# A decoder step on one core: layer 0's second token half by seven block products in 19 of its 22 FFN slices, their operand sums in tiles that attention outputs held, those outputs through DRAM, and the memory tokens loaded one stage earlier

## The chip, the core and the metric

The kernel runs on one NeuronCore of a Trainium2 chip. The metric is the device time of one execution in microseconds (us); lower is better. Five engines run their own instruction lists in order and wait for each other by semaphores: PE (TensorE, matmuls and transposes; "PEld" in the profile is its weight loading), DVE (VectorE), ACT (ScalarE), POOL (GpSimd, which here issues copies from DRAM to DRAM) and SP (SyncE, which issues nearly all other DMAs).

## What is computed

One inference step of a two-layer decoder over two groups of tokens with the same weights: a prompt of 1024 tokens and 8 sample tokens. The width is 1024, everything is float32.

```python
for l in (0, 1):
    hn = rmsnorm(h, g[0])
    # layer 0: gated linear recurrence; layer 1: stick-breaking attention over a shared K/V
    # both: in parallel with cross-attention into 256 memory tokens
    mix = concat(mixer(hn), mem_attend(q_m, mem_k[l], mem_v[l])) @ w_o[l]
    h = h + rmsnorm(mix, g[1])
    h = h + rmsnorm(swiglu(rmsnorm(h, g[2]), w_gu[l], w_down[l]), g[3])
    if l == 0:                                  # shared K/V, used by layer 1
        sb_k, sb_v = split(rmsnorm(h, g_kv) @ w_kv)
# swiglu(x) = (silu(x @ w_gate) * (x @ w_up)) @ w_down, hidden width 22 * 128 = 2816
```

The memory keys and values are projected from `mem_prompt` for both layers. Outputs are the hidden states of both groups, the recurrent states, the shared K/V and the memory K/V.

## The kernel before

**Tiles.** Activations lie transposed, channels on the 128 partitions and tokens along the free dimension. The prompt is cut in two halves: group 0 has 512 tokens, group 1 has 512 plus the 8 sample tokens, 520 columns taken as two pieces of 260. A float32 product is made of three matmuls in a reduced format (fp32r): each operand is split into a high part, rounded by ACT, and a low part, the remainder from DVE (`split_w`, lines 206 and 207, for weights; `split_to` for activations), and high*high, high*low and low*high are summed in PSUM.

**Two ways to make an FFN slice.** The hidden width is worked in 22 slices of 128, numbered 0 to 21 and grouped into five parts of 5, 5, 4, 4 and 4 (`PARTS`). A slice needs a gate and an up projection over 1024 channels, then SiLU and a product; at the end of a part the down projection adds its share to `R`.

- Plain (class `ffn`, through `proj`, line 220; or `gate_up_q`, line 464, inside `ffn_w`): for each of gate and up, 8 channel blocks by 3 terms by 2 pieces, 96 matmuls a slice.
- Seven block products (`gate_up_w`, line 511): the 2 x 2 block form by Strassen's scheme in Winograd's variant. The channels are halved, the tokens are halved, gate and up are the two output blocks. Seven products of 4 channel blocks by 3 terms, 84 matmuls a slice, on sums of weights and sums of activations. Four PSUM banks `pa`, `pb`, `pc`, `pd` (one buffer each) hold the partial sums, and ACT copies a partial sum with its sign turned from `pa` to `pb` after the first product and from `pb` to `pc` after the third. The weight sums of a part are made ahead in DRAM by POOL's accumulating DMAs (`weight_sums`, lines 549 to 569): 16 for a part, in two runs of eight of which most must wait for an earlier one to land. Each is preceded by a tiny POOL copy (`mk`) that reads the tile in `now[0]`; it paces the DMAs by the work. The activation sums are made by `sums_w` in 16 steps during the first slices of the class, which are plain (the `steps` argument); a slice by products needs 7 weight tiles split, a plain one 4.

SiLU is done either by ACT's `Silu` (in `gate_up_q` and `gate_up_w`) or as Exp, Ln, Exp and a DVE product (`silu`, lines 237 to 241). The second form needs no other function table than the softmax and the stick-breaking attention do.

**Order.** The program is one sequence of Python generators. `weave` advances several of them in turn, each in proportion to the number given with it; a scheduler then orders each engine's list, and tiles come from pools with a fixed number of buffers, so that a new tile waits until the last reader of an old one is through. The stages that matter here, in the main part at the end of `tile_decoder`:

1. `a0.v()` and `a0.fq()` project for group 0; then `a0.core()`, the recurrence, is woven with `mem_load()` (memory tokens transposed and split, lines 796 to 814), the memory keys and values of both layers, and `a0.qm`.
2. Later, `f0.finish`, `kv_proj(0)`, `b0.heads()` and `o1.finish()`: end of layer 0 for group 0, shared K/V, layer 1's queries for group 0, and the residual and norm that give group 1 its FFN input `o1.x` (while `o1.R` keeps the same values unsplit).
3. `b0.sb()` and `b0.mem()`, layer 1's two attentions of group 0, woven with parts 0 and 1 of group 1's layer 0 FFN by class `ffn`, plain. The attention outputs go to the eight `xo` tiles taken by `b0.open()` from pool `xpool` (tag `x0`, 8 buffers) and are split there (lines 911, 912, 1404, 1405).
4. `set_banks(True)` changes PSUM from two double banks to four single ones, and `ffn_w(1, 0, ...)` makes parts 2 to 4: slices 10 to 12 plain, slices 13 to 21 by products. Its operand sums lie in pool `apool`.
5. `o0.mm(b0.xo, ...)`: the output projection of layer 1 for group 0.

Layer 1's own weight sums (`ws`) are spread over many of these stages.

Of the kernel before, what the change touches and what calls it, by code (L numbers as in the profile page):

```python
# [9 lines left out]
F32 = mybir.dt.float32  # L10
# [8 lines left out]
P = 128  # L19
# [4 lines left out]
def tile_decoder(  # L24
# [11 lines left out]
    H = 4  # L36
# [189 lines left out]
    def split_to(dst, src):  # L226
        nc.scalar.copy(dst[0], src)  # L227
        nc.vector.tensor_sub(dst[1], src, dst[0].bitcast(F32))  # L228

    def silu(dst, ps, g):  # L230


        n = NG[g]
        x = T()
        dst = T() if dst is None else dst
        d = dst[:, :n]
        nc.vector.tensor_scalar(sv(x, g), pv(ps, g), -44.0, None, op0=ALU.max)  # L237
        nc.scalar.activation(d, x[:, :n], AF.Exp, scale=-1.0)
        nc.scalar.activation(d, d, AF.Ln, bias=1.0)
        nc.scalar.activation(d, d, AF.Exp, scale=-1.0)  # L240
        nc.vector.tensor_mul(d, d, x[:, :n])
        return dst
# [35 lines left out]

    def sums_w(g, xs, ops, YT, ZT):

# [4 lines left out]
        for k in range(4):  # L285
# [14 lines left out]

            b11, b12, b21, b22 = full(x0, 0), full(x0, h), full(x1, 0), full(x1, h)
            for d, p, a, b in (
# [148 lines left out]

    def gate_up_q(g, l, f, xt, side, n_side, first):

# [3 lines left out]
        for j in range(2):  # L457
# [14 lines left out]
            for a in range(2):  # L472
                d = sg[:, a * h : (a + 1) * h]
                if j == 0:
# [6 lines left out]

    def gate_up_w(g, l, f, ops, spl, raws):

# [39 lines left out]
        sg = T()  # L523
        nc.scalar.activation(sg[:, :h], pa[:, :h], AF.Silu)
        product(pb, 4)
        dt = T()
        nc.scalar.copy(dt[:, h:n], pd[:, :h])
        gt = T()
        nc.vector.tensor_add(gt[:, h:n], dt[:, h:n], pb[:, :h])
        product(pc, 5)  # L530
        nc.vector.tensor_sub(gt[:, :h], pc[:, :h], dt[:, h:n])
        product(pb, 6)
        act[0] = nc.scalar.activation(sg[:, h:n], gt[:, :h], AF.Silu)
        nc.vector.tensor_mul(sg[:, :h], sg[:, :h], pb[:, :h])  # L534
# [40 lines left out]
    class ffn_w:  # L575


        def __init__(self, g, l, x, steps, first, rows, R=None, own=False):
# [3 lines left out]
            self.half = []  # L582

            def YT():
# [6 lines left out]
            self.sums = sums_w(g, x, self.ops, YT, YT if rows else lambda: A(F32R))  # L591

        def spl(self):
            self.n += 1
            if (self.pi or not self.rows) and not self.own and self.n % 8 in (1, 4, 6):
                return cpool.tile([P, 2, 512], F32R, tag="c", name=nm("ws"))
# [8 lines left out]
        def raws(self):  # L605
            self.r += 1
            if not self.rows and self.r % 2:
                return B().rearrange("p (k m) -> p k m", k=4)
# [7 lines left out]
        def part(self, pi):  # L616
# [5 lines left out]
            for j in range(nf):  # L622
                self.pi = pi
                if f0 + j < self.plain:
                    mids.append(
                        gate_up_q(g, l, f0 + j, self.x, self.sums, self.steps[j], PARTS[self.first][0])
                    )
                    now[0] = mids[-1][:, 0, 0:1].bitcast(F32)
                else:
                    mids.append(gate_up_w(g, l, f0 + j, self.ops, self.spl, self.raws))  # L630
                yield
# [232 lines left out]
    def mem_attn(g, l, qm, xo):  # L864
# [4 lines left out]
        for h in range(H):  # L869
            po = S()  # L870
            for pr in range(2):
# [38 lines left out]
                yield  # L910
            d = xo[H + h]
            split_to((d[:, 0, :G], d[:, 1, :G]), po)

# [426 lines left out]
    def sb_prompt(g, Qs, xo):  # L1340
# [49 lines left out]
        for h in range(H):  # L1390
# [12 lines left out]
            values(vh, po, *late)  # L1403
            d = xo[h]
            split_to((d[:, 0, :G], d[:, 1, :G]), po)

# [17 lines left out]
    class mixer_b:  # L1424
# [6 lines left out]

        def open(self):
            self.xo = wo_tiles(self.g)

# [40 lines left out]
    with tc.issue_after(made[0].ins):  # L1475
# [160 lines left out]
```

## Time and profile before

| | |
|---|---|
| time, median of 3 runs | 2454.28 us (2452.27 to 2455.25) |
| the profiled execution | 2454.5 us, its span 2452.8 us |
| PE busy | 2413.3 us, 98% of the span, 15839 matmuls recorded |
| DVE, ACT, POOL busy | 1639.9, 1252.4 and 187.0 us |
| DMA | 397.40 MB, mean 162 GB/s; SP's queue 43.2%, POOL's 14.2% of the span of 16 DMA engines |
| granted TensorE clock | 0.998 |

The 1.7 us between the profiled execution's time and its span lie around the program. In a row of a timeline the first number is the start from the span's start, the second the length of a merged group, the number after "x" the count; text in square brackets tells how long the engine was idle before and what released it. A group can be drawn longer than the distance to the next one, since matmuls overlap: times between starts are the ones to use. In a row of groups stand busy time, mean ns of one instruction, and idle time before it. In a row of windows stand, for each engine, busy time and number of instructions, then the granted clock, the DMA share and GB/s. An engine with a "q" (SPq) is that engine's queue of issuing instructions.

### The profile page before, as it was taken

The numbers are of one execution on the slowest core, as the hardware profiler recorded it, in microseconds if no ns is written. First come the engines' busy times: TensorE is split into PE (matmuls) and PEld (weight loads), VectorE is DVE, ScalarE is ACT, GpSimd is POOL, SyncE is SP. The second block draws the span as 40 slices with busy tenths as digits, with TensorE's granted clock in tenths as the row PEclk, the third lists the DMA queues.
The fourth block names the chain that finished last, engine by engine and source line by source line (L and its number), as shares of the span: only waits on it lengthen the run. The fifth ranks groups of instructions, "written<-read, shape, count | busy, mean of one in ns | idle before, by whom it ended". The sixth has DMA issues, their size and how long they took to land.

```text
span 2452.8 us, 42098 instructions
## 1 busy us (share of the span) xinstructions
PE 2413.3 (98%) x15839; PEld 2161.2 (88%) x15839; DVE 1639.9 (67%) x2987; ACT 1252.4 (51%) x2441; POOL 187.0 (8%) x315
## 2 busy tenths in 40 slices
PE   8999999999999999999999999999999999999998
PEld 6888889888879988999999989877777888999998
DVE  5766557665797686664756685788688467755565
ACT  5547644354445554555434554555554445654445
POOL 1000101111000000111200102121000100000000
PEclk9999999999999999999999999999999999999999
DMA  6354676567645447676766649745354563464542
GB/s 190 100 174 110 157 197 161 135 171 204 204 137 166 132 147 235 176 188 161 190 172 168 199 132 291 206 146 154 95 164 120 145 191 116 144 194 141 151 143 74
DMA packets 534733, 397.40 MB, mean 162 GB/s; under 512 B 21325, under 2 KB 473018, under 8 KB 534530
## 3 DMA queue, kind: packets, MB, share of 16 engines
q1 hardware_dynamic: 505346, 315.02, 43.2%
q0 software_dynamic: 29184, 79.70, 14.2%
q8 instruction: 124, 2.03, 0.3%
q14 instruction: 79, 0.65, 0.1%
HBM read 364.81 MB, written 101.14 MB: 190 GB/s over the span
## 4 chain that ended last, share of the span: by engine, by line
PE 84%; DVE 6%; DMA 5%; issue 2%; ACT 2%; POOL 0%; SPq 0%; DVEq 0%; ACTq 0%; POOLq 0%
PE mm L220 44%; PE q L511 13%; PE q L648 9%; PE q L464 3%; PE mm L1042 2%; PE s L1188 1%; DMA c<-in_cache_mem_v 1%; PE s L1385 1%; PE s L906 1%; PE mm L824 1%; PE mm L851 1%; PE q L680 1%; PE s L1351 1%; PE s L875 1%; DVE ws L207 1%
## 5 line engine op out<-in xcount | busy, mean ns | idle before, releaser
L220 PE MATMUL mm<-x,ws 128*128 128x260 f32 (+1 forms) x6240 | 1113.6, 335 | 4.9 <-DVE t L237 1.7
L220 PEld LDWEIGHTS mm<-x,ws 128*128 128x128 f32 x6240 | 941.8, 188 | 125.8 <-issue 2.4
L206 ACT CAST ws<-w 128x512 fp32r<-128x512 f32 (+1 forms) x652 | 382.3, 588 | 489.5 <-PE mm L220 337.0
L207 DVE TENSOR_TENSOR ws<-w,ws 128x512 fp32r<-128x512 f32 (+1 forms) x652 | 418.9, 648 | 246.8 <-ACT ws L206 241.7
L220 PE MATMUL mm<-m,ws 128*128 128x512 f32 (+1 forms) x1344 | 281.8, 361 | 0.1
L220 PEld LDWEIGHTS mm<-m,ws 128*128 128x128 f32 x1344 | 217.9, 189 | 36.8 <-issue 1.0
L648 PE MATMUL q<-m,ws 128*128 128x260 f32 (+1 forms) x1824 | 221.8, 283 | 0.0
L648 PEld LDWEIGHTS q<-m,ws 128*128 128x128 f32 x1824 | 218.9, 188 | 1.2 <-DVE t L534 0.4
L502 DVE TENSOR_TENSOR ws<-w,ws 128x512 fp32r<-128x512 f32 x181 | 124.0, 690 | 86.6 <-ACT ws L501 83.6
L501 ACT CAST ws<-w 128x512 fp32r<-128x512 f32 x181 | 111.8, 621 | 110.2 <-PE q L648 35.6
L511 PE MATMUL q<-x,ws 128*128 128x260 f32 (+1 forms) x1188 | 158.1, 282 | 0.0
L511 PEld LDWEIGHTS q<-x,ws 128*128 128x128 f32 x1188 | 148.7, 188 | 0.0
L511 PE MATMUL q<-y,ws 128*128 128x260 f32 x912 | 119.7, 284 | 0.4 <-ACT q L521 0.3
L511 PEld LDWEIGHTS q<-y,ws 128*128 128x128 f32 x912 | 113.7, 189 | 0.8 <-ACT q L521 0.5
L464 PE MATMUL q<-x,ws 128*128 128x260 f32 (+1 forms) x720 | 91.3, 284 | 0.2 <-DVE r L400 0.2
L464 PEld LDWEIGHTS q<-x,ws 128*128 128x128 f32 x720 | 88.4, 189 | 1.8 <-DVE r L400 0.5
L511 PE MATMUL q<-a,ws 128*128 128x260 f32 (+1 forms) x672 | 87.0, 282 | 0.0
L511 PEld LDWEIGHTS q<-a,ws 128*128 128x128 f32 x672 | 83.2, 188 | 0.0
L657 DVE TENSOR_TENSOR r<-r,q 128x260 f32<-128x260 f32 (+1 forms) x128 | 48.5, 420 | 50.5 <-PE q L648 50.5
L237 DVE TENSOR_SCALAR t<-mm 128x512 f32<-128x512 f32 (+1 forms) x58 | 40.1, 691 | 48.0 <-PE mm L220 47.8
L563 POOL COPY mk<-a 128x1 f32<-128x1 f32 x36 | 21.3, 592 | 645.5 <-ACT a L1241 392.9
L228 DVE TENSOR_TENSOR m<-t,m 128x512 fp32r<-128x512 f32 (+1 forms) x88 | 60.8, 691 | 9.4 <-ACT m L227 8.7
(355 smaller groups left out, 3029.5 us busy)
## 6 DMA issues: line engine op xcount, KB each, us to landing
w<-in_w_gu SPq DMA_DIRECT2D x297, 256.0 KB
w<-in_w_down SPq DMA_DIRECT2D x160, 256.0 KB
wsum<-in_w_gu POOLq DMA_DIRECT2D x72, 512.0 KB, 6.6
w<-wsum SPq DMA_DIRECT2D x104, 256.0 KB
w<-in_w_in_a SPq DMA_DIRECT2D x80, 256.0 KB
w<-in_w_o SPq DMA_DIRECT2D x64, 256.0 KB
wsum<-in_w_gu POOLq DMA_DIRECT2D x24, 640.0 KB, 7.3
wsum<-wsum POOLq DMA_DIRECT2D x24, 512.0 KB, 5.7
```

The costliest lines, as they stand in the source:

```text
L206: nc.scalar.copy(ws[:, 0, :n, :], raw[:, :n, :])
L207: nc.vector.tensor_sub(ws[:, 1, :n, :], raw[:, :n, :], ws[:, 0, :n, :].bitcast(F32))
L220: nc.tensor.matmul(ps[:, a, : PW[g]], wt, xt[k][:, xi, o : o + PW[g]], start=(k == 0 and wi == 0), stop=(k == nk - 1 and wi == 2),)
L228: nc.vector.tensor_sub(dst[1], src, dst[0].bitcast(F32))
L237: nc.vector.tensor_scalar(sv(x, g), pv(ps, g), -44.0, None, op0=ALU.max)
L464: ins = nc.tensor.matmul(pp[a][:, :h], wt, xt[k][:, xi, a * h : (a + 1) * h], start=(k == 0 and wi == 0), stop=(k == ND - 1 and wi == 2),)
L501: nc.scalar.copy(w[:, 0, :], src)
L502: nc.vector.tensor_sub(w[:, 1, :], src, w[:, 0, :].bitcast(F32))
L511: nc.tensor.matmul(ps[:, :h], w[:, wj, k * P : (k + 1) * P], x[:, xi, :], start=(first and k == 0 and wi == 0), stop=(k == 3 and wi == 2), ...
L648: nc.tensor.matmul(pp[a][:, :h], wt, mids[k][:, xi, a * h : (a + 1) * h], start=(k == 0 and wi == 0), stop=(k == nf - 1 and wi == 2),)
L657: nc.vector.tensor_add(d, d, pp[a][:, :h])
L1042: nc.tensor.matmul(pb[i][:, a, :], xt[k][:, xi, c * P : (c + 1) * P], ws[:, s, :], start=(k == 0 and wi == 0), stop=(k == ND - 1 and wi == 2),
```

## The change

Group 1's layer 0 FFN is now made by `ffn_w` throughout: slices 0 to 2 plain by `gate_up_q`, slices 3 to 21 by seven products, so that ten slices (3 to 12) change from 96 to 84 matmuls and need 7 instead of 4 weight splits. What that takes:

- Weight sums of layer 0's parts 0 and 1 (`w1`): 32 more DMAs by POOL of 640 KB each, issued while `f0.finish`, `kv_proj(0)` and `b0.heads()` run.
- The single PSUM banks hold from the start of stage 3 on. The first two parts run beside the attentions (`beside=(0, 1)`). There the SiLU takes the form with Exp and Ln (`lean`), where it works on both token halves at once after the sixth product, and weight tiles come from `wraw` and `wspl` alone (5 buffers each).
- The activation sums are made in place from `o1.R` (`src`), without the 16 additions of `full`, and lie in the eight `x0` tiles.
- Group 0's attention outputs therefore go unsplit to DRAM (`put`: an ACT copy, a store by SP), and `mixer_b.load` brings them back and splits them during the last down projection.
- `mem_load()` is woven with `a0.fq()`, one stage earlier.

```diff
+    def put(xo, i, cols, src):
+        if isinstance(xo, list):
+            split_to((xo[i][:, 0, cols], xo[i][:, 1, cols]), src)
+            return
+        t = B()[:, : cols.stop - cols.start]
+        nc.scalar.copy(t, src)
+        nc.sync.dma_start(xo[:, i, cols], t)
...
     # sums_w(..., src=None)
+            if src:
+                b11, b12, b21, b22 = (src[i][:, c : c + h] for i in (k, k + 4) for c in (0, h))
+            else:
+                b11, b12, b21, b22 = full(x0, 0), full(x0, h), full(x1, 0), full(x1, h)
...
+    def gated(d, x):
+        nc.scalar.activation(d, x, AF.Exp, scale=-1.0)
+        nc.scalar.activation(d, d, AF.Ln, bias=1.0)
+        nc.scalar.activation(d, d, AF.Exp, scale=-1.0)
+        nc.vector.tensor_mul(d, d, x)
...
     # gate_up_q(..., lean=False)
+                if j == 0 and lean:
+                    if a == 0:
+                        x = T()
+                    nc.vector.tensor_scalar(x[:, a * h : (a + 1) * h], pp[a][:, :h], -44.0, None, op0=ALU.max)
+                    if a:
+                        gated(sg[:, :n], x[:, :n])
+                elif j == 0:
...
     # gate_up_w(..., lean=False)
         product(pa, 3)
         sg = T()
+        if lean:
+            nc.vector.tensor_scalar(sg[:, :h], pa[:, :h], -44.0, None, op0=ALU.max)
+        else:
+            nc.scalar.activation(sg[:, :h], pa[:, :h], AF.Silu)
         product(pb, 4)
         dt = T()
+        if lean:
+            gt = dt
+            nc.scalar.copy(dt[:, :h], pd[:, :h])
+            nc.vector.tensor_add(gt[:, h:n], dt[:, :h], pb[:, :h])
+            product(pc, 5)
+            nc.vector.tensor_sub(sg[:, h:n], pc[:, :h], dt[:, :h])
+            nc.vector.tensor_scalar(sg[:, h:n], sg[:, h:n], -44.0, None, op0=ALU.max)
+            x, sg = sg, T()
+            product(pb, 6)
+            gated(sg[:, :n], x[:, :n])
...
         nc.vector.tensor_mul(sg[:, :h], sg[:, :h], pb[:, :h])
         nc.vector.tensor_mul(sg[:, h:n], sg[:, h:n], gt[:, h:n])
...
     # ffn_w(..., beside=(), src=None)
-                if rows:
+                if rows or beside:
                     return xpool.tile([P, 2, NG[1]], F32R, tag="x0", name=nm("y"))
...
     # mem_attn
-            d = xo[H + h]
-            split_to((d[:, 0, :G], d[:, 1, :G]), po)
+            put(xo, H + h, slice(0, G), po)
     # sb_prompt
-            d = xo[h]
-            split_to((d[:, 0, :G], d[:, 1, :G]), po)
+            put(xo, h, slice(0, G), po)
...
+        def load(self):
+            d, n, self.xo = self.xo, NG[self.g], []
+            for k in range(ND):
+                t = T()
+                nc.sync.dma_start(t[:, :n], d[:, k, :n])
+                x = X(self.g)
+                split_to((x[:, 0, :n], x[:, 1, :n]), t[:, :n])
+                self.xo.append(x)
+                yield
...
-    drain(a0.v(), a0.fq())
+    drain(a0.v())
+    weave((a0.fq(), 8), (mem_load(), 2))
     weave(
         (a0.core(), 22),
-        (chain(mem_load(), mem_keys(0), mem_values(0), mem_keys(1), mem_values(1), a0.qm(M)), 22),
+        (chain(mem_keys(0), mem_values(0), mem_keys(1), mem_values(1), a0.qm(M)), 20),
     )
...
+    w1 = weight_sums(0, (0, 1))
     drain(o1.mm(a1.xo, 0, 1))
-    weave((f0.finish(True), 9), (o1.mm(a1.xo, 1, 5), 4))
-    weave((normed(0, f0.R, f0.r, gkvcol, xk0, True), 8), (o1.mm(a1.xo, 5, 7), 2))
-    drain(kv_proj(0, xk0))
-    weave((normed(0, f0.R, f0.r, lambda k: gcol(1, 0, k), xb0), 8), (o1.mm(a1.xo, 7, ND), 1))
+    weave((f0.finish(True), 9), (o1.mm(a1.xo, 1, 5), 4), (islice(w1, 8), 9))
+    weave((normed(0, f0.R, f0.r, gkvcol, xk0, True), 8), (o1.mm(a1.xo, 5, 7), 2), (islice(w1, 4), 5))
+    weave((kv_proj(0, xk0), 8), (islice(w1, 10), 11))
+    weave((normed(0, f0.R, f0.r, lambda k: gcol(1, 0, k), xb0), 8), (o1.mm(a1.xo, 7, ND), 1), (islice(w1, 4), 5))
     b0 = mixer_b(0, xb0)
-    weave((b0.heads(), 8), (o1.finish(), 17), (islice(ws, 4), 4))
-    b0.open()
+    weave((b0.heads(), 8), (o1.finish(), 17), (w1, 6))
+    b0.open(True)
+    set_banks(True)
+    fw = ffn_w(1, 0, o1.x, (5, 6, 5), 0, False, beside=(0, 1), src=o1.R)
+    weave((chain(b0.sb(), b0.mem()), 25), (chain(fw.part(0), fw.part(1)), 18), (islice(ws, 34), 35))
+    p4 = fw.part(4)
+    weave((chain(fw.part(2), fw.part(3), islice(p4, 4)), 20), (islice(ws, 12), 12))
+    weave((p4, 4), (b0.load(), 8))
     f1 = ffn(1, 0, o1.x)
-    weave((chain(b0.sb(), b0.mem()), 25), (chain(f1.part(0), f1.part(1)), 18), (islice(ws, 34), 35))
-    set_banks(True)
-    fw = ffn_w(1, 0, o1.x, (5, 6, 5), 2, False, f1.R)
-    weave((chain(fw.part(2), fw.part(3), fw.part(4)), 24), (islice(ws, 8), 8))
-    f1.acc = fw.acc
+    f1.R, f1.acc = fw.R, fw.acc
     set_banks(False)
```

More of the change, by code (lines that the diff above doesn't have):

```diff
@@ L575, in tile_decoder, with __init__ @@
     class ffn_w:
-        def __init__(self, g, l, x, steps, first, rows, R=None, own=False):
+        def __init__(self, g, l, x, steps, first, rows, R=None, own=False, beside=(), src=None):
             self.g, self.l, self.x, self.ops, self.steps, self.rows, self.own = g, l, x, [], steps, rows, own
@@ L582, in __init__ @@
             self.half = []
+            self.beside = beside
             def YT():
-                if rows:
+                if rows or beside:
                     return xpool.tile([P, 2, NG[1]], F32R, tag="x0", name=nm("y"))
@@ L589, in YT @@
                 return A(F32R)
-            self.sums = sums_w(g, x, self.ops, YT, YT if rows else lambda: A(F32R))
+            self.sums = sums_w(g, x, self.ops, YT, YT if rows or beside else lambda: A(F32R), src)
         def spl(self):
             self.n += 1
-            if (self.pi or not self.rows) and not self.own and self.n % 8 in (1, 4, 6):
+            if (self.pi or not self.rows) and not self.own and self.pi not in self.beside and self.n % 8 in (1, 4, 6):
                 return cpool.tile([P, 2, 512], F32R, tag="c", name=nm("ws"))
@@ L606, in raws @@
             self.r += 1
-            if not self.rows and self.r % 2:
+            if not self.rows and self.pi not in self.beside and self.r % 2:
                 return B().rearrange("p (k m) -> p k m", k=4)
@@ L625, in part @@
                     mids.append(
-                        gate_up_q(g, l, f0 + j, self.x, self.sums, self.steps[j], PARTS[self.first][0])
+                        gate_up_q(
+                            g, l, f0 + j, self.x, self.sums, self.steps[j], PARTS[self.first][0], pi in self.beside
+                        )
                     )
```

30 lines of the change are left out of this document (14 added, 16 removed).

## The prediction

> **What bounds the kernel now.** I read the page first: the span, the busy shares, and the chain of work that ended last.
>
> ```profile
> span 2452.8 us, 42098 instructions
> ...
> PE 2413.3 (98%) x15839; PEld 2161.2 (88%) x15839; DVE 1639.9 (67%) x2987; ACT 1252.4 (51%) x2441; POOL 187.0 (8%) x315
> ...
> PE 84%; DVE 6%; DMA 5%; issue 2%; ACT 2%; POOL 0%; SPq 0%; DVEq 0%; ACTq 0%; POOLq 0%
> ```
>
> PE is busy 98% of the span, and 84% of the last chain is PE. Whoever takes matmuls away shortens the kernel, as long as the other engines still deliver. The second view is the table of windows over the stretches that the change touches: the start with the memory tokens, the stretch that gets the new weight sums, stage 3 (attentions beside parts 0 and 1), parts 2 to 4, and a later stretch; the last row is a stretch of it that is full of POOL's sums.
>
> ```profile
> 0.00:300.00 300.00, 284.82 (x1723) 247.97 (x1724) 198.52 (x423) 171.38 (x353) 19.85 (x56) 0.99 0.50 143
> ...
> 852.00:998.00 146.00, 144.73 (x831) 124.39 (x832) 103.87 (x170) 74.97 (x132) 5.32 (x8) 1.00 0.61 182
> 998.00:1216.00 218.00, 217.34 (x1686) 207.11 (x1686) 133.31 (x262) 113.33 (x230) 35.00 (x65) 1.00 0.71 174
> 1216.00:1411.00 195.00, 194.72 (x1622) 194.08 (x1620) 114.16 (x211) 91.06 (x175) 18.71 (x27) 1.00 0.67 187
> 1411.00:1560.00 149.00, 145.69 (x1011) 133.96 (x1012) 106.41 (x177) 75.86 (x134) 24.05 (x36) 1.00 0.77 217
> ...
> 1005.00:1105.00 100.00, 99.51 (x780) 93.98 (x779) 60.11 (x108) 54.79 (x106) 16.08 (x32) 1.00 0.71 179
> ...
> 1471.00:1533.00 62.00, 60.81 (x480) 58.46 (x480) 34.81 (x61) 27.06 (x47) 13.09 (x22) 1.00 1.05 292
> ```
>
> In stage 3 PE idles 0.66 us of 218, in parts 2 to 4 0.28 of 195: there is nothing to win there but matmuls, and any new wait is paid in full. At the start PE idles 15.2 us of 300.
>
> **Matmuls.** The third view is PE's timeline: a piece of a plain slice woven with attention, then a plain slice and a slice by seven products in parts 2 to 4.
>
> ```profile
> 1129.31 8.14 PE L220 MATMUL mm<-x,ws 128*128 128x260 f32 x65
> 1137.29 1.03 PE L875 MATMUL s<-c,a 128*128 128x256 f32 x4
> ...
> 1221.75 28.86 PE L464 MATMUL q<-x,ws 128*128 128x260 f32 x240
> 1250.44 1.60 PE L511 MATMUL q<-x,ws 128*128 128x260 f32 x12
> ...
> 1283.72 1.61 PE L511 MATMUL q<-x,ws 128*128 128x260 f32 x12
> 1285.16 3.04 PE L511 MATMUL q<-a,ws 128*128 128x260 f32 x24
> ...
> 1293.79 1.59 PE L511 MATMUL q<-x,ws 128*128 128x260 f32 x12
> ```
>
> Start to start, a woven matmul takes (1137.29 - 1129.31) / 65 = 0.1228 us, an unwoven plain one (1250.44 - 1221.75) / 240 = 0.1195. One product, 12 matmuls, takes 1285.16 - 1283.72 = 1.44 us, and a slice by products (1293.79 - 1283.72) = 10.07 us for 84. Slices 3 to 12 lose 12 matmuls each, 120 in all, and the order of the two kernels' instructions on PE shows exactly 120 fewer. That is -14.4 us at 0.12; if the woven matmuls (some 590 in seven slices) also came down from 0.1228 to 0.1195, -2 more. I take **-15** (-14.4 to -17).
>
> **Memory tokens.** The waits of PE at `mem_load` and just behind it:
>
> ```profile
> 87.77 0.63 PE L807 MATMUL ns<-ident,c 128*128 128x128 f32 x4 [2.60 <-DVE memt L228]
> ...
> 89.06 2.93 PE L1168 MATMUL s<-b,a 128*128 128x192 f32 x8 [0.66 <-ACT b L1164]
> ...
> 93.02 0.51 PE L824 MATMUL mm<-memt,ws 128*128 128x256 f32 x2 [0.46 <-ACT memt L227]
> 93.72 1.22 PE L824 MATMUL mm<-memt,ws 128*128 128x256 f32 x8 [0.19 <-DVE memt L228]
> ```
>
> The transposes wait for the splits of the ones before. Woven with `a0.fq()` they have projection matmuls ahead of them in PE's list. The four waits add to 3.9 us; the 16 transposes only move, and the splits lie beside matmuls. What could be late next is the 0.66 that has an ACT instruction of the recurrence behind it, so I take **-3** (0 to -3.9).
>
> **The new form of SiLU.** This is where the change can lose. In a slice by products in parts 2 to 4 the sixth partial sum leads to one DVE subtraction and one ACT `Silu`, then two DVE products free the banks:
>
> ```profile
> 1292.55 0.43 DVE L531 TENSOR_TENSOR t<-q,t 128x260 f32<-128x260 f32 x1
> ...
> 1293.13 0.42 ACT L533 ACTIVATE t<-t 128x260 f32<-128x260 f32 x1
> ...
> 1294.20 0.42 DVE L534 TENSOR_TENSOR t<-t,q 128x260 f32<-128x260 f32 x1
> ...
> 1295.42 0.37 ACT L518 ACTIVATE q<-q 128x260 f32<-128x260 f32 x1
> ```
>
> Bank `pb` is read last by the first product (L534 before, 571 after), and the next slice's sign copy (L518 before, 541 after) must write `pb`, which the next slice's third product needs. Before, the reader starts 1.65 us after the subtraction and no wait of PE follows. In the seven slices of parts 0 and 1 (3 to 9) that reader is instead behind a longer chain. The durations, from the groups by form:
>
> ```profile
> L531 DVE TENSOR_TENSOR t<-q,t 128x260 f32<-128x260 f32 x28 | 12.0, 428 | 2.6 <-PE q L511 1.9
> ...
> L524 ACT ACTIVATE t<-q 128x260 f32<-128x260 f32 x28 | 10.8, 387 | 16.2 <-PE q L511 16.2
> ...
> L239 ACT ACTIVATE t<-t 128x512 f32<-128x512 f32 x32 | 20.2, 632 | 1.0
> ...
> L241 DVE TENSOR_TENSOR t<-t,t 128x512 f32<-128x512 f32 x32 | 22.1, 689 | 24.4 <-ACT t L240 24.4
> ...
> L501 ACT CAST ws<-w 128x512 fp32r<-128x512 f32 x181 | 111.8, 621 | 110.2 <-PE q L648 35.6 <-PE q L511 25.8 <-DMA w<-wsum 18.7
> L502 DVE TENSOR_TENSOR ws<-w,ws 128x512 fp32r<-128x512 f32 x181 | 124.0, 690 | 86.6 <-ACT ws L501 83.6 <-DMA w<-wsum 1.1 <-DMA w<-in_w_down 0.4
> ```
>
> After the sixth product (`pc`): subtraction 0.43, clamp (an SBUF operation, between 0.35 and 0.43; 0.35), Exp, Ln, Exp at 0.63 each on all 520 columns, the product of sigmoid and gate 0.69, the product with `pb` 0.43, the sign copy 0.37: 4.16. One weight cast of ACT (0.62) will stand between two of them, since casts keep coming: 4.78; nine hand-overs between engines at about 0.1 (1293.13 less the 1292.98 at which L531 ends is 0.15) make 5.7. What PE has meanwhile is the seventh product and the next slice's first two, 3 x 1.44, and, woven in, part of an attention unit, about 0.4: 4.7. So PE waits about **1.0** at each hand-over, and there are seven: slice 3 to 4, 4 to the down projection, 5 to 6, 6 to 7, 7 to 8, 8 to 9, 9 to the down projection. That is **+7**. The low end is 0: the weave can put a score product of 1.03 us there. The high end is a queue on ACT and DVE: the softmax's exponentials stand in the same ACT list, and so does their accumulator reading.
>
> ```profile
> L886 ACT ACTIVATE b<-s,nmx 128x256 f32<-128x256 f32 x64 | 29.9, 471 | 18.0 <-DVE nmx L880 17.8
> ...
> L886 ACT ACTIVATION_READ_ACCUMULATOR b<-s,nmx 128x1 f32 x64 | 12.6, 197 | 0.0
> ...
> L892 DVE TENSOR_SCALAR b<-b,sme 128x256 f32<-128x256 f32 x64 | 19.9, 352 | 0.7
> ```
>
> Two of these with their readings, 1.34, and a further cast, 0.62, add 1.9 to the 1.0: 2.9 at each, +20. I keep 0 to 20.
>
> **The plain slices 0 to 2.** The sums are made here: 16 steps of a subtraction (0.43) and a split (its DVE half as long) are 13.7 us of DVE in three slices of 96 x 0.1228 = 11.8 plus 1.7 of attention, 40.5 us. DVE is busy 0.60 of the row 1005 to 1105, 24.3 of 40.5; with the sums 38.0, 94%. It fits, barely. And there are fewer PSUM buffers for scores now, since the first gate pieces take two of the tag `S`. I take **+2** (0 to 5, the high end being three waits for a softmax round of 0.47 + 0.20 + 0.35 with its scores' hand-overs, about 1.6 each).
>
> **The weight sums `w1`.** 32 DMAs of 640 KB enter 852 to 998, where 4 sum DMAs of `ws` go out. A run of eight by POOL, with the queue's totals:
>
> ```profile
> q0 software_dynamic: 29184, 79.70, 14.2%
> ...
> 1466.68 0.60 POOL L568 DMA_DIRECT2D wsum<-in_w_gu  x1 [0.27 <-issue]
> ...
> 1498.59 0.87 POOL L566 DMA_DIRECT2D wsum<-in_w_gu  x1 [3.31 <-DMA wsum<-wsum]
> ```
>
> Eight take 32 us, four runs 128: from 852 they end at about 980. Slice 3 needs the first two runs at 998 + 40 = 1038, slice 5 the other two at about 1100. Late sums are thus unlikely. But the stretch fills: its 0.61 of 146 us is 89 us of DMA, and 28 more DMAs at 14.2% of 2452.8 us over 120 sum DMAs (2.9 us each) add 81, 170 of 146. The row 1471 to 1533 shows such a stretch, share 1.05 and 292 GB/s, and there PE idles 1.19 of 62 us, 1.9%; over 146 us that is 2.8, against 1.27 there now. So **+2** (0 to 6; the overflow mostly drags the sums, which have time).
>
> Parts 0 and 1 also ask SP for 21 more weight tiles of 256 KB, 5.5 MB, in the stage at 174 GB/s: some 38 more, 212, no more than 1411 to 1560 carries (217).
>
> **Outputs through DRAM.** `put` is an ACT copy and a store in place of an ACT copy and a DVE remainder of 0.69: DVE gains 8 x 0.69. `load` makes eight casts and eight remainders, 8 x (0.62 + 0.69) = 10.5 us on two engines, beside a last down projection of 192 x 0.12 = 23 us: 0 (0 to 2, the last tile's landing and split if it trails).
>
> **Slices 10 to 12 by products** behave like slices 13 to 21 now, which have no PE wait to speak of (0.28 us of 195): nothing beside their 36 matmuls. Their sums are in place before.
>
> **Sum,** against the profiled execution's own 2454.5 us (span 2452.8 and 1.7 around it; the median of the runs is 2454.28, 0.2 less): -15 - 3 + 7 + 2 + 2 = -7, 2447.5; on the median's scale **2447**.
>
> **Rivals.**
> 1. *Nothing is lost.* Hand-overs, sums and DMA stay hidden: 2454.5 - 18 = 2436.5. For it: PE's 0.4 of attention at each hand-over is an estimate and may be a whole unit. Against it: the chain of 5.7 us is longer than the three products in any case.
> 2. *All is eaten.* 1.7 at each hand-over (one more cast and some queueing), 3 in the plain slices, 3 from DMA: 12 + 6 = 18, so 2454.5. For it: DVE at 94% there.
> 3. *Slower.* At each of the seven hand-overs the sign copy on ACT or the product on DVE stands behind a whole softmax or stick-breaking round. Even with gain 18 and 4 elsewhere, it turns at (18 - 4) / 7 = 2.0 us each; with 3.3 (the 2.9 above and DVE's 0.35 of L892) it is 7 x 3.3 + 4 = 27, +9, 2463.5. For it: ACT and DVE run in list order, so one early attention instruction that waits for PE holds the chain, and PE waits for the chain. Against it: ACT is busy only 0.55 of 1005 to 1105.
> 4. *The clock falls.* If short waits between groups made the granted clock 0.75 through seven slices of 10.07: 7 x 10.07 x (1 / 0.75 - 1) = +23.5, about 2470. The windows speak against it: 0.99 in 0 to 300 with 15.2 us of idle PE, 1.00 in 1411 to 1560 with 3.3. The Trainium skill, "TensorE: Matmul & The Clock Gate", section "A second HAM failure mode: psum-queue depth-cycling", tells of a kernel whose PE idled briefly between groups while it cycled through PSUM banks, and whose clock swung between half and full rate; by that rule this form, which cycles four banks, would be such a case. The parts 2 to 4 cycle the same four banks at 1.00, so the trace bears it out only for a PE that doesn't wait.
>
> That the change doesn't do what it says is excluded for the matmuls by the count of 120.
>
> **How the numbers follow.** Forecast 0.54 (hand-overs at 0 to 1.6 each, 2439 to 2451); nothing lost 0.10; all eaten 0.18; slower 0.15; clock 0.02; late sums or something else 0.01. The range 2437 to 2461 takes the forecast, the eaten case, nearly all of the first and a part of the third. About 0.2%, 4.9 us, is what a measurement of this kernel can tell from no change: faster is below 2449.4, slower above 2459.2. The forecast gives 0.49 to faster and 0.05 to the middle, rival 1 all to faster, rival 2 most to the middle (0.01 to slower): faster 0.59, same 0.22, slower 0.19.
>
> **What would show it.** In the profile after: 120 fewer matmuls; no wait on `memt`; slices 3 to 9 at 10.1 us plus attention, with PE's waits on the sign copy (ACT, line 541) about 1 us at each hand-over, and those of the plain slices 2 us together; POOL's last `w1` sum before 1038; PE's idle time in 852 to 998 below 4 us; eight `load` splits before the output projection's first matmul; the granted clock at 1.00. Waits of 2 us and more at line 541 would make it wrong upwards, none would make it wrong downwards.

## The result

The changed kernel takes 2481.65 us (median of 6 runs, 2477.54 to 2487.32) where the kernel before takes 2455.08 in the same comparison: a ratio of 1.0109 (95% interval 1.0094 to 1.0124), 26.6 us slower. The forecast was 2447, with a range up to 2461. The profiled execution, 2487.3 us with a span of 2485.5, was the slowest of the six, so distances within its trace are a few microseconds larger than those between medians.

The page of the changed kernel, the lines that answer to those shown of before:

```profile
span 2485.5 us, 42261 instructions
...
PE 2414.0 (97%) x15719; PEld 2156.4 (87%) x15719; DVE 1658.7 (67%) x3049; ACT 1278.4 (51%) x2517; POOL 228.2 (9%) x379
...
q0 software_dynamic: 35840, 100.68, 17.5%
...
PE 79%; DMA 8%; DVE 7%; ACT 3%; issue 3%; SPq 1%; POOL 0%; DVEq 0%; ACTq 0%; POOLq 0%
```

The 120 matmuls are gone (15839 to 15719), yet PE's busy time is the same, 2414.0 us after 2413.3; and the idle time has grown from 39.5 to 71.5 us. So the remaining matmuls have become slower, by 0.7 + 14.4 = 15 us in all (120 matmuls at 0.12 us are the 14.4). The mean granted clock agrees, 0.991 after 0.998. DMA's share of the last chain has gone from 5% to 8%.

Where it went is read by four landmarks on PE's timeline, which both kernels have: the group of 227 matmuls after group 0's first FFN, the first score matmuls of the attentions, the first matmul of slice 10, and the output projection of layer 1. Of the kernel before:

```profile
858.87 27.31 PE L220 MATMUL mm<-x,ws 128*128 128x260 f32 x227
...
997.60 1.03 PE L1351 MATMUL s<-a,a 128*128 128x128 f32 x4
...
1216.02 5.89 PE L464 MATMUL s<-x,ws 128*128 128x260 f32 x48
...
1411.61 5.80 PE L220 MATMUL mm<-x,ws 128*128 128x512 f32 x24 [0.90 <-DVE r L657]
```

and of the changed kernel:

```profile
851.80 27.31 PE L220 MATMUL mm<-x,ws 128*128 128x260 f32 x227
...
1012.09 1.03 PE L1390 MATMUL s<-a,a 128*128 128x128 f32 x4
...
1236.54 2.66 PE L534 MATMUL q<-x,ws 128*128 128x260 f32 x12 [2.56 <-DVE r L697]
...
1440.52 5.77 PE L220 MATMUL mm<-x,ws 128*128 128x512 f32 x24 [0.90 <-DVE r L697]
```

| stretch, us | before | changed | difference | forecast |
|---|---|---|---|---|
| start to the 227 matmuls | 858.9 | 851.8 | -7.1 | -3 |
| 227 matmuls to the attentions (where `w1` is made) | 138.7 | 160.3 | +21.6 | +2 |
| attentions to slice 10 (parts 0 and 1) | 218.4 | 224.5 | +6.0 | -10.3 matmuls, +7, +2 |
| slice 10 to the output projection (parts 2 to 4) | 195.6 | 204.0 | +8.4 | -4.3 |
| the rest | 1041.2 | 1045.0 | +3.8 | 0 |

The windows of the changed kernel over the second, third and fourth stretch, and over 13 us of the second:

```profile
852.00:1012.00 160.00, 142.22 (x778) 119.55 (x777) 103.10 (x172) 73.64 (x131) 31.03 (x54) 0.96 0.98 268
1012.00:1236.00 224.00, 213.78 (x1606) 202.43 (x1604) 140.53 (x297) 129.11 (x283) 36.20 (x68) 0.98 0.85 219
1236.00:1440.00 204.00, 196.11 (x1584) 194.27 (x1584) 124.46 (x234) 100.76 (x196) 22.60 (x32) 0.97 0.72 198
...
955.00:968.00 13.00, 4.69 (x14) 3.22 (x15) 1.35 (x4) 0.62 (x1) 2.51 (x4) 0.61 1.07 341
```

The DMA share of the second stretch is 0.98 (0.61 before). In 955 to 968 all 16 DMA engines are busy, PE works 4.69 of 13 us, and the granted clock there is 0.61. PE's waits in this stretch, from the view of waits:

```profile
PE ns L391 <- DMA ht<-in_x_prompt: 9.5, 2, 6.8
PE ns L264 <- ACT n L227: 6.7, 3, 3.3
```

The first is the prompt's rows arriving late from DRAM (issued at 955.4 to 957.7, 7.9 us to land). The second names ACT; but ACT's own list shows what held it ahead of PE's waits at 950 and 990, casts of weight tiles that had not landed:

```profile
946.69 0.62 ACT L206 CAST ws<-w 128x512 fp32r<-128x512 f32 x1 [6.15 <-DMA w<-in_w_in_b]
...
987.85 0.62 ACT L206 CAST ws<-w 128x512 fp32r<-128x512 f32 x1 [3.46 <-DMA w<-in_w_in_b]
```

The issues by line of that stretch give these weights a median of 13.4 us from issue to landing:

```profile
w<-in_w_in_b SPq DMA_DIRECT2D x16, 256.0 KB, 13.4
```

**So the first theory (A)** was: the weight-sum DMAs fill the DMA engines, what SP loads comes late, engines that work their lists in order pass the delay on, and PE pays twice, by the wait and by a slower clock behind it. **The rival (B)**, the forecast's own fear, was the chain of the new SiLU at the hand-overs between slices and the fuller lists of DVE and ACT.

### The profile page after: what moved, and what is told of

It is laid out like the page before. It is cut to its first block, busy times and chain, and to the rows that moved or that the text cites. A ratio compares the mean times of both kernels' runs of the same rounds, so it can differ in the third digit from the quotient of the medians.

```text
span 2485.5 us, 42261 instructions
## 1 busy us (share of the span) xinstructions
PE 2414.0 (97%) x15719; PEld 2156.4 (87%) x15719; DVE 1658.7 (67%) x3049; ACT 1278.4 (51%) x2517; POOL 228.2 (9%) x379
## 4 chain that ended last, share of the span: by engine, by line
PE 79%; DMA 8%; DVE 7%; ACT 3%; issue 3%; SPq 1%; POOL 0%; DVEq 0%; ACTq 0%; POOLq 0%
PE mm L220 36%; PE q L534 16%; PE q L688 10%; PE q L481 3%; DMA w<-in_w_in_b 2%; PE s L1227 1%; PE mm L1081 1%; DVE ws L207 1%; PE s L946 1%; PE s L1424 1%; DMA w<-in_w_gu 1%; PE mm L891 1%; PE mm L864 1%; PE q L720 1%; PE s L1390 1%
## 5 line engine op out<-in xcount | busy, mean ns | idle before, releaser
L220 PE MATMUL mm<-x,ws 128*128 128x512 f32 (+1 forms) x5280 | 993.5, 344 | 4.1 <-DVE r L697 1.7
L220 PEld LDWEIGHTS mm<-x,ws 128*128 128x128 f32 x5280 | 825.1, 189 | 123.7 <-DVE x L228 2.1
L206 ACT CAST ws<-w 128x512 fp32r<-128x512 f32 x612 | 357.5, 586 | 469.5 <-PE mm L220 279.2
L207 DVE TENSOR_TENSOR ws<-w,ws 128x512 fp32r<-128x512 f32 x612 | 391.5, 645 | 253.2 <-ACT ws L206 246.6
L688 PE MATMUL q<-m,ws 128*128 128x260 f32 (+1 forms) x2304 | 290.2, 286 | 9.1 <-DVE r L697 9.1
L688 PEld LDWEIGHTS q<-m,ws 128*128 128x128 f32 x2304 | 282.4, 191 | 12.9 <-DVE r L697 7.2
L534 PE MATMUL q<-y,ws 128*128 128x260 f32 x1824 | 246.1, 286 | 3.3 <-ACT q L541 3.1
L525 DVE TENSOR_TENSOR ws<-w,ws 128x512 fp32r<-128x512 f32 x241 | 165.5, 690 | 117.8 <-ACT ws L524 115.1
L534 PEld LDWEIGHTS q<-y,ws 128*128 128x128 f32 x1824 | 230.5, 190 | 5.1 <-ACT q L541 4.4
L220 PE MATMUL mm<-m,ws 128*128 128x512 f32 x864 | 219.8, 402 | 0.7 <-DVE r L411 0.7
L524 ACT CAST ws<-w 128x512 fp32r<-128x512 f32 x241 | 148.8, 619 | 135.1 <-PE q L688 40.1
L603 POOL DMA_DIRECT2D wsum<-in_w_gu x80 | 73.0, 924 | 163.1 <-DMA wsum<-wsum 124.6
L228 DVE TENSOR_TENSOR m<-t,m 128x512 fp32r<-128x512 f32 (+1 forms) x88 | 60.8, 690 | 10.1 <-ACT m L227 8.5
```

Source lines behind the costliest of these rows:

```text
L206: nc.scalar.copy(ws[:, 0, :n, :], raw[:, :n, :])
L207: nc.vector.tensor_sub(ws[:, 1, :n, :], raw[:, :n, :], ws[:, 0, :n, :].bitcast(F32))
L220: nc.tensor.matmul(ps[:, a, : PW[g]], wt, xt[k][:, xi, o : o + PW[g]], start=(k == 0 and wi == 0), stop=(k == nk - 1 and wi == 2),)
L524: nc.scalar.copy(w[:, 0, :], src)
L525: nc.vector.tensor_sub(w[:, 1, :], src, w[:, 0, :].bitcast(F32))
L534: nc.tensor.matmul(ps[:, :h], w[:, wj, k * P : (k + 1) * P], x[:, xi, :], start=(first and k == 0 and wi == 0), stop=(k == 3 and wi == 2), ...
```

## The experiments

**One part alone, on the kernel before.**

Memory tokens, with `weave((a0.fq(), 8), (mem_load(), 2))` and nothing else:

> The kernel before with one edit: the memory tokens woven with a0.fq(). All theories: the four PE waits of 3.9 us at the memory tokens go, and the clock that the profile shows at 0.99 in the first 300 us goes back to 1.00, so 4 to 7 us faster than before, some 2448 us. If the 7.1 us that the changed kernel is ahead at the end of group 0's first FFN came from elsewhere, it would be faster by less than 3.

Measured: 2448.53 us, ratio 0.9973 (0.9960 to 0.9985). So the 7 us are this move. Its window of the first 300 us:

```profile
0.00:300.00 300.00, 289.00 (x1748) 251.31 (x1749) 198.97 (x425) 172.90 (x357) 23.17 (x62) 1.00 0.52 149
```

PE is idle 11.0 us there after 15.2, so 4.2 of the 7 are the waits. The clock reads 1.00 after 0.99: before, it was 0.84 in 86 to 90 us and 0.73 in 90 to 94, and 1.00 in both with the move. PE was busy 1.57 and 3.35 us of these, so an estimated 0.16 x 1.57 + 0.27 x 3.35 = 1.2 us more. In the traces the 227 matmuls start 5.7 us earlier.

Weight sums, issued as in the changed kernel and read by nobody:

```diff
+    w1 = weight_sums(0, (0, 1))
...
-    weave((f0.finish(True), 9), (o1.mm(a1.xo, 1, 5), 4))
+    weave((f0.finish(True), 9), (o1.mm(a1.xo, 1, 5), 4), (islice(w1, 8), 9))
...
```

> The kernel before with one edit: the 32 weight-sum DMAs of parts 0 and 1 are issued where the changed kernel issues them (and ws is spread as there), though nothing reads them. Theory A (the DMA engines are full in that stretch; weights and prompt rows come late, PE waits, and the granted clock falls after each wait): 16 to 24 us slower than before, about 2475, with the loss between the end of group 0's FFN and the start of the attentions. Rival B (the hand-overs between slices and the fuller DVE and ACT lists cost the time): within 3 us of before.

Measured: 2477.78 us, ratio 1.0090 (1.0072 to 1.0108), 22 us slower. The trace is of the fastest of the four runs, 17 us longer than that of before:

```profile
859.11 27.31 PE L220 MATMUL mm<-x,ws 128*128 128x260 f32 x227
...
1014.12 1.14 PE L1351 MATMUL s<-a,a 128*128 128x128 f32 x4 [0.17 <-DMA a<-ksc]
```

The stretch before the attentions takes 155.0 us, 16.3 more than before, and the next stretch 218.5, as before: the loss is where theory A put it. B is out for this part, since no slice has changed.

Half of these sums, 16 at half the pace:

> The kernel before with the weight-sum DMAs of part 0 alone, 16 in place of 32, at half the pace over the same stages; nothing reads them. Theory A in its form with a threshold (PE waits only where the DMA engines are full, and 0.61 of 146 us and 12 more DMAs of 2.9 us stay at 0.85): 0 to 5 us slower than before, 2455 to 2460. In its form without one (each sum DMA costs its share, 22 us for 32): 11 us slower, about 2466.

Measured: 2460.02 us, ratio 1.0015 (1.0004 to 1.0026), some 4 us (1 to 6 by the interval). Sixteen cost some 4 and thirty-two 22, so the price isn't proportional to the count. Whether there is a threshold, two counts can't tell. The same window as in the forecast, in the traces of the half and of the whole change:

```profile
852.00:998.00 146.00, 144.23 (x827) 123.28 (x825) 102.76 (x168) 74.89 (x132) 21.14 (x31) 1.00 0.84 236
```
```profile
852.00:998.00 146.00, 128.22 (x718) 108.15 (x717) 89.30 (x147) 64.82 (x115) 27.45 (x50) 0.95 1.00 275
```

At a share of 0.84 PE works 144.23 of 146 us, at 1.00 it works 128.22. The half does lose something just behind this window: PE's first score matmuls wait 2.88 us at 999.8 for keys from DRAM (`a<-ksc`).

Attention outputs through DRAM (`put` and `load`, with the weave of the last part):

> The kernel before with one edit: the attention outputs go through DRAM and are loaded back and split during the last down projection. Theory A, whose second part is that a split waits on ACT for its load and holds the next weight splits and the additions to R behind it: 5 to 10 us slower than before, with one PE wait of 4 us or more at the last down projection. Rival B: within 2 us of before.

Measured: 2461.04 us, ratio 1.0022 (1.0010 to 1.0034), 5.6 us slower by the medians; slice 10 to the output projection takes 201.2 us after 195.6. The wait at the last projection is 2.63, smaller than expected, and 144 matmuls behind it take 20.30 us, where 144 x 0.12 is 17.3.

**The changed kernel with fewer or other sums.**

18 of the 32 sums one stage earlier, woven with `rest()`:

> The changed kernel with 18 of the 32 weight-sum DMAs moved one stage earlier, beside layer 0's group 0 FFN, and 14 left where they were. Theory A: the stretch before the attentions gives back 12 to 20 of its 21.6 us, and the time is 2462 to 2470. Rival B: no gain beyond 3 us, 2478 or more.

Measured: 2470.95 us, 10.7 less than the changed kernel and just above what theory A gave. The stretch before the attentions is back to 139.2 us with its 14 sums, but the 227 matmuls start at 863.6, 10.4 later than with the memory tokens alone (853.2): 18 sums in a stretch that has DMA shares of up to 0.69 without them cost 10.4 there (7.4 and 9.8 in the two runs below that issue them in the same place). A page that shows a mean share of 0.4 to 0.7 for a stretch does not show that it has room.

No sums at all for parts 0 and 1 (`w1 = iter(())`, the products read the sums of other parts):

> The changed kernel without the 32 weight-sum DMAs: the products of parts 0 and 1 read the sums of parts 2 and 3 in their place (this leaves the right operands out; the loads are of the same size and count). Theory A: 20 to 24 us less than the changed kernel, 2457 to 2462, since the rest of the change (load wait, crowded stage 3) stays. Rival B: under 5 us less.

Measured: 2467.51 us, 14.1 less than the changed kernel by the medians (22 by the two traces). Less than expected by the medians; and still 12 us slower than before, though memory tokens and matmuls should give 21 and the outputs cost 5.6. The stretch before the attentions is 138.8, attentions to slice 10 takes 220.4, slice 10 to the output projection 204.9. Thus parts 0 to 4 lose also without the sums of parts 0 and 1.

The same, and 24 of the 34 layer 1 sums moved out of that stage into layer 1's attentions of group 1:

```diff
-    ... (islice(ws, 34), 35))
+    ... (islice(ws, 10), 11))
...
-        (chain(f0.part(0), f0.part(1), f0.part(2), islice(p3, 4)), 30),
+        (chain(f0.part(0), f0.part(1), f0.part(2), islice(p3, 4)), 30), (islice(ws, 24), 25),
```

> As the run without the 32 weight-sum DMAs, and 24 of layer 1's moved out of the stage with parts 0 and 1. Theory A: 6 to 12 us less than that run, 2447 to 2455: with both crowds of DMA gone, the ten slices by products show what they save, apart from the load wait. Rival B: no less than 2457, as the hand-overs still cost what they did.

Measured: 2475.09 us, 7.6 more, not less. The trace splits it: attentions to slice 10 falls from 220.4 to 213.4 us, as theory A has it, and behind the output projection the time rises from 1046.8 to 1068.7. The sums, or what they hold up, cost more where they were moved to.

The same move on a kernel with all its sums, 18 of them earlier:

> As the run with loads two ahead, and 24 of the 34 layer 1 weight-sum DMAs that run beside the attentions and parts 0 and 1 are moved to layer 1's attentions of group 1. Theory A: PE's waits at the down projections of parts 0 and 1 (9.5 and 5.0 us put down to the additions to R, in truth late weights) go, 8 to 14 us less; some of it is paid where the DMAs go now; 2452 to 2460. Rival B (the chain of the SiLU and full DVE and ACT lists hold PE in that stage): within 3 us of the run with loads two ahead.

Measured: 2482.08 us, 10.5 more than the run it is compared with (loads two ahead, below, 2471.59). Again the stage gains 9.4 (223.9 to 214.5 us) and the rest loses 18.9 (1044.8 to 1063.7). Whether that loss is DMA at all was not taken apart: PE's waits there are put down to ACT and DVE of the attentions, and the mean DMA share there is only 0.58.

Slices 10 to 12 alone by products, which need no new weight sums:

```diff
-    fw = ffn_w(1, 0, o1.x, (5, 6, 5), 0, False, beside=(0, 1), src=o1.R)
+    fw = ffn_w(1, 0, o1.x, (2,) * 8 + (0, 0), 0, False, beside=(0, 1), src=o1.R)
```

> The changed kernel with slices 0 to 9 plain, so that only slices 10 to 12 change to products, and without the 32 weight-sum DMAs, which nothing needs then; the activation sums are made over slices 0 to 7. Theory A: what is left of the change is the memory tokens (-7), 36 matmuls (-4.3) and the load (+5.6 to +9): 2449 to 2454. Rival B (the lean SiLU and the sums in full DVE and ACT lists cost the time): over 2458.

Measured: 2474.78 us, a clear miss: over 20 us above the expectation. Attentions to slice 10 takes 228.9 us, 10 more than before, although no slice of it changed its count of matmuls. PE's waits in that stage are below 0.5 us each up to its last one, so the new SiLU of the plain slices isn't it (its form in the slices by products doesn't occur in this run). The last one is 6.9:

```profile
1212.08 0.62 ACT L524 CAST ws<-w 128x512 fp32r<-128x512 f32 x1 [5.91 <-DMA w<-wsum]
1212.60 0.29 ACT L206 CAST ws<-w 128x128 fp32r<-128x128 f32 x1
...
1213.34 0.76 DVE L697 TENSOR_TENSOR r<-r,q 128x260 f32<-128x260 f32 x2
...
1213.90 6.09 PE L688 MATMUL q<-m,ws 128*128 128x260 f32 x30 [6.93 <-DVE r L697]
```

ACT's list has a cast of slice 10's first weights (L524) ahead of the cast that the projection of part 1 still needs (L206). Slice 10's tile comes 5.9 us late, so ACT waits, DVE behind it, and PE behind both; the projection's own tile had been there. In 1190 to 1225 the issues by line give 10.1 us to land for these tiles. With the 30 matmuls behind it, which take 5.9 us from start to start where 3.6 is usual, this wait is 9.2 of the 10 us. The changed kernel has the same at 1220 to 1237 (PE waits of 2.14 and 2.56 us). Another 6 us are lost behind the output projection of this run; PE waits of 4.8 and 2.7 us there are put down to DVE, and their cause stays open.

**The load at the last down projection.** The changed kernel's largest wait is there, and the same pattern:

```profile
1418.29 0.62 ACT L227 CAST x<-t 128x512 fp32r<-128x512 f32 x1 [8.02 <-DMA t<-xo]
1418.81 0.61 ACT L206 CAST ws<-w 128x512 fp32r<-128x512 f32 x1
...
1419.55 0.76 DVE L697 TENSOR_TENSOR r<-r,q 128x260 f32<-128x260 f32 x2
...
1420.02 4.39 PE L688 MATMUL q<-m,ws 128*128 128x260 f32 x18 [5.76 <-DVE r L697]
```

ACT is idle for 8 us until the first loaded output lands; its issue, at 1407.38, stands behind loads of 520 KB (`ht<-hs`) that took 11.6 us to land. Three attempts at it:

> The changed kernel with 18 of its 32 weight-sum DMAs one stage earlier, as in the run before, and each load of an attention output issued two ahead of the split that reads it. Theory A: the PE wait of some 5 us at the last down projection, with the slower clock behind it, mostly goes; 4 to 8 us less than the 2471 of the run without it, so 2463 to 2467. Rival (that wait comes from weights that land late, not from the order of load and split): within 2 us of 2471.

Measured: 2471.59 us, no change from 2470.95.

> The changed kernel; the first three loads of attention outputs are issued ahead of the last down projection as now, but no split of one stands in ACT's and DVE's lists before half of that projection is through. Theory A (a split that waits for its load on ACT holds the weight splits and the additions to R behind it, whatever the order of issue): the wait of 5.8 us and the slow clock behind it go, 5 to 9 us less than the changed kernel, 2473 to 2477. Rival (the weights of that projection are themselves late): within 3 us of 2482.

Measured: 2484.07 us, no change from the changed kernel, with the wait still there (6.32). Both prove nothing about the theory: the scheduler orders each engine's list by itself, and in ACT's list of both kernels the splits stand where they stood. The order of the generators doesn't decide it. The last attempt ties each split to an ACT instruction of the projection:

```diff
-                split_to((x[:, 0, :n], x[:, 1, :n]), ts[k][:, :n])
+                with tc.issue_after(sqi[0].ins):
+                    split_to((x[:, 0, :n], x[:, 1, :n]), ts[k][:, :n])
```

(`sqi[0]` is the latest square, for the first split that of the fourth block). On the outputs alone and on the changed kernel:

> The kernel before with the attention outputs through DRAM, and the splits of the loaded outputs held in ACT's list behind the square of the last down projection's fourth block. If ACT's order makes the wait: within 2 us of before, some 4 us less than the 2461 of the outputs alone, and no wait of over 1 us at the last down projection. If the weights themselves are late: 2461 again, with the same wait. If the splits are now too late: a wait of some us ahead of the output projection.

> The changed kernel with the splits of the loaded outputs held in the same way. If ACT's order makes the wait: 5 to 9 us less than the changed kernel, 2473 to 2477, and slice 10 to output projection in 195 to 199 us in place of 204. If not: 2480 or more, and 204 us.

Measured: 2458.63 us, ratio 1.0013 (1.0004 to 1.0023), 2.4 less than the outputs alone, but 4.2 above the kernel before in the same comparison, where at most 2 were expected; and 2475.32 us, ratio 1.0091 (1.0074 to 1.0109), 6.3 less than the changed kernel, as expected. In both pairs the intervals overlap, so the times alone don't prove the gain. The traces do: slice 10 to the output projection takes 197.0 and 196.6 us, after 201.2 and 204.0 (204.2 in the run before, which has the same loads without the tie). In the changed kernel with the tie the weight casts of the last projection stand ahead of the splits:

```profile
1401.99 0.62 ACT L206 CAST ws<-w 128x512 fp32r<-128x512 f32 x1 [1.22 <-PE q L690]
...
1417.60 1.65 ACT L227 CAST x<-t 128x512 fp32r<-128x512 f32 x3
...
1424.34 6.67 PE L220 MATMUL mm<-x,ws 128*128 128x512 f32 x21 [2.31 <-DVE r L699]
```

The waits at the last projection are gone in both, and one of 2.2 to 2.3 us is left ahead of the output projection. The order of ACT's list made the wait.

**Three slices with this load later** (before the order was known to stand):

> As the run with slices 10 to 12 alone, with the splits of the loaded outputs later as in the first of these. Theory A: without the load wait 2443 to 2448, no slower than the 2448.5 of the memory tokens alone. Rival: no better than the run with slices 10 to 12 alone.

Measured: 2476.09 us, no better than 2474.78, as follows from the list that had not changed.

**The best version** is the memory tokens alone, 2448.53 us, 0.27% faster than the kernel before; no run with products in more slices came near it. No run held slice 10's casts back as the splits were held, so what the change would give with its sums, its load and these casts all mended isn't measured.

## Why the prediction was wrong

Step by step, with the differences of the two traces (that of the changed kernel is its slowest run, 5.7 us above the median):

- **Matmuls, -15: the count was right, the gain was not kept.** 120 went, and the lower clock took the 15 us back. The forecast took 0.12 us a matmul for granted, from stretches in which PE never waited.
- **Memory tokens, -3: mis-sized, -7.** The four waits did go; the forecast left out that the matmuls around them had run at a granted clock of 0.84 and 0.73.
- **Weight sums, +2 (0 to 6): this is the term that failed, at +21.6 in the trace.** Three other traces with all 32 sums in this stretch have +15.8 to +17.2; by the medians the sums cost 14 to 22 us. The sum of DMA time, 170 us in 146, was near enough (the kernel before has 128 sum DMAs and not 120, which makes 2.7 us each and 165), and so was the remark that POOL's chain would be dragged: the last of `w1`, the 32nd sum DMA from 845 on, is issued at 1009.6 and not at about 980, which is still before slice 3. The step that failed came next: the price of a full stretch was taken from 1471 to 1533, where PE idles 1.9% at a share of 1.05. That row shows a stretch in which PE hardly had to wait for its loads; it doesn't bound one in which PE waits for the prompt's rows and ACT for the queries' weights. The estimate from the other side stood in the same line, 170 - 146 = 24 us, and belonged in the range. In place of the +2 it gives 2469, still short, for the other two omissions below.
- **Hand-overs of the new SiLU, +7, and plain slices, +2: too high.** PE's waits on the sign copy are 2.8 us in this stretch, 2.6 of them at one hand-over, and at the plain slices PE waits 0.4. At that hand-over, at 1144, the list went as rival 3 feared (two exponentials of a softmax and casts between the chain's steps), but once, not seven times; two other runs with this stretch have two such waits, of 1.5 to 3.0 us. With 24 layer 1 sums and `w1` out of the way, attentions to slice 10 takes 213.4 us where 218.4 - 10.3 = 208.1 would be free of any loss: 5.3 us are all that hand-overs, plain slices and the rest cost.
- **Parts 0 and 1, DMA at +0: an omission.** The 21 extra tiles were found to fit a mean of 212 GB/s (219 measured), and that was taken for free. (5.5 MB over the 218 us of the stretch is 25 GB/s and not 38; nothing hangs on it.) The stretch lost 16.3 us against the matmuls' 10.3 that it should have gained. Of these 7.0 go when 24 of layer 1's sums leave it (220.4 to 213.4; 9.4 in the other pair), and 5.3 are left then. The 4.1 between are no measure of `w1`, which ends before the stretch: with the same sums the stretch took 226.4 and 220.3 us in two other runs. Nor are the extra tiles of slices 3 to 9 shown to be the cause: with these slices plain the stretch still lost 10.4 us, nearly all of it at slice 10's late tiles.
- **Outputs, 0 to 2: the step that failed is "beside a last down projection of 23 us".** The engines' time was counted and the order was not: a split that waits for its load stands in ACT's list ahead of a weight cast, and the projection waits for that. Tied behind, 7.4 us of the 12.7 lost in this stretch are gone. Of the other 5.3, the slow start at slice 10 is 1.6 and the longer wait ahead of the output projection (2.31 us after 0.90) 1.4; the rest wasn't taken apart.
- **The rest, +3.8:** one wait of 5.7 us for keys from DRAM (`a<-ksc`), which is 1.0 before; its cause stays open.
- **The rivals.** Rival 3, slower by waits at the hand-overs, had 0.15 (0.19 for slower in all); the sign came true by another mechanism. Rival 4, the clock, named an effect that did appear, of another size and from another cause: the clock is 0.98 in parts 0 and 1 and not 0.75, and where it was read closely it fell behind waits of 2 us and more, not behind short ones between banks. After the two at 1226 and 1234 the changed kernel's timeline and windows read

```profile
1236.54 2.66 PE L534 MATMUL q<-x,ws 128*128 128x260 f32 x12 [2.56 <-DVE r L697]
1239.00 3.61 PE L534 MATMUL q<-y,ws 128*128 128x260 f32 x24
1242.45 1.61 PE L534 MATMUL q<-x,ws 128*128 128x260 f32 x12
1243.90 1.61 PE L534 MATMUL q<-y,ws 128*128 128x260 f32 x12
...
1229.00:1232.00 3.00, 3.00 (x20) 3.00 (x20) 1.06 (x2) 0.00 (x0) 0.00 (x0) 0.67 1.03 370
1237.00:1240.00 3.00, 3.00 (x16) 3.00 (x15) 2.80 (x6) 1.17 (x3) 0.00 (x0) 0.50 1.12 206
1240.00:1244.00 4.00, 4.00 (x34) 4.00 (x33) 1.81 (x3) 2.08 (x5) 0.00 (x0) 0.97 1.12 277
```

The first 12 take 2.46 us from start to start, the next 24 take 3.45, the following 12 the usual 1.45: 36 matmuls lose 1.6 us beside the wait itself. The granted clock is 0.67 and 0.50 behind the two waits, with PE busy throughout, and 0.97 from 1240 on. The Trainium skill, "TensorE: Matmul & The Clock Gate", section "Part 1: The HAM clock gate (the "warmup" mystery)", says that an idle window of about 3.4 us returns the array to half rate, and that the window runs free of the kernel. The trace agrees that the clock falls behind idle time, but not with the length: the two waits here, of 2.14 and 2.56 us and some 8 us apart, are shorter than the page's window and were enough, and the measurement decides.

## What to carry to other kernels

Where PE is busy 98%, a change that buys matmuls with DMA has to be priced by the DMA engines of each stretch: added and existing transfer time against the stretch's length. The whole excess belongs in the range, and neither a mean share of 0.6 nor one full stretch that happened not to wait is a comfort. No excess doesn't mean no price: 18 sums in a stretch whose mean share stayed at 0.73 with them cost 7 to 10 us. A load whose consumer stands early in the list of a busy engine can be as dear as a wait on PE itself; see in the engine's list what stands behind it, and check after an edit that the list has changed. A wait of some 2 us on PE cost more than its length here, for the matmuls behind it ran slower.

## What the runs showed of the hardware

- What added DMA costs is not proportional to its amount: 16 sums at a share of 0.84 cost some 4 us, 32 at 0.98 to 1.00 cost 14 to 22, and the queries' weight tiles of 256 KB then took a median of 13.4 us to land.
- The granted clock was 0.61 over 13 us in which PE was busy 4.69, and 0.50 to 0.67 behind two waits of 2.14 and 2.56 us while PE was busy throughout. Over the whole change the clock cost about 15 us (2414.0 us for 15719 matmuls after 2413.3 for 15839), as much as the 120 matmuls had been expected to give.
- A cast that waits for its tile in ACT's list holds the casts behind it. ACT's list shows that ahead of PE waits of 5.76 and 6.93 us; with the splits tied behind the weight casts the first was gone, the second wasn't put to a test.
